# A hybrid two-layer backbone: the norms between the layers traced behind part of the next block's MLP products, and the first two projection groups ordered by block

## The chip, the cores and the metric

The kernel runs on one core of one Trainium2 chip. The metric is the device time of one execution in microseconds; the time shown is a median over several executions, and one further execution was profiled. PE is TensorE, ACT is ScalarE, DVE is VectorE, POOL is GpSimd, SP is the engine that issues most transfers.

## The reference

1,280 tokens (256 of context, then 1,024 latent ones) of width 1,024 pass through two layers. The reference in outline:

```python
for l in range(2):
    mod = silu(c) @ ada_w[l] + ada_b[l]          # shifts, scales, gates; one set for latent, one for context
    h = rms_norm(x, norm1_g[l]) * (1 + sc1) + sh1
    z = h @ w_in[l]                              # the projections: columns for four mixers
    mix = concat(s5(z), mlstm(z), diff_attention(z), gla(z)) @ w_out[l]
    x = x + g1 * mix
    h2 = rms_norm(x, norm2_g[l]) * (1 + sc2) + sh2
    x = x + g2 * (square(relu(h2 @ mlp_w1[l])) @ mlp_w2[l])
return rms_norm(x_latent, final_norm_g)
```

## The kernel before, in words

**Layout.** The stream X is kept with the 1,024 features on partitions (eight tiles of 128) and the tokens along the row, in three blocks: b0 is the context (tokens 0 to 255), b1 and b2 are 512 latent tokens each. Every float32 product is three products of reduced-precision halves (hi by hi, lo by hi, hi by lo: lines 1126 to 1128), so each weight tile is split into whi (a cast on ACT, line 1117) and wlo (a subtraction on DVE, line 1118), and each activation into hhi and hlo.

**Between the layers.** In the last pass of layer 0's MLP (w2, products named m2p) the blocks come in the order b1, b2, b0 (LAST). For each block there are G = 2 loads of weights, and M = 4 outputs for each load, of six matmuls each. Before the change, when a block's eight outputs are done, its X is stored (xl_d) and it is normed for layer 1 at once: block_rstd squares the eight tiles on ACT (nsq, line 1183), sums them on PE with eight small products (np4, line 1185), copies (line 1187), spreads by one product (npm, line 1189) and takes the inverse root (lines 44 to 49). norm_block then makes hhi and hlo: for odd tiles POOL multiplies (line 1201), ACT scales and casts (1205, 1206) and DVE subtracts (1207); for even tiles DVE multiplies (1210), ACT casts (1211) and DVE subtracts (1212).

**The projections.** z_steps goes through a list of groups (ZORD). In layer 0 the first are dak1, dak2, daq1; in layer 1 s50, s51, dak1. Each group has one weight tile of 128 columns and makes, per block, 24 matmuls into one PSUM bank (zp; the tag has two buffers), which ACT copies out into a tile "zst" and stores. The tiles zst, nsq and nt (line 1210) share one tag of two buffers. Before, a group passes over all blocks (b0, b1, b2 in layer 0; b1, b2, b0 in layer 1) before the next group. In layer 0 the norm of the blocks is traced between the split of the first group's weights and the first products, and rows of the modulation (adap, adar, lines 1161 to 1172) are woven in. `ready(("dak1",))` traces groups until the named one is done; after it the S5 mixer's preparation (s5_prep) is traced.

**What sets the order.** Each engine works through its instructions in order. The order on PE is not simply the traced order: PE's instructions are moved ahead or behind by a scheduler when the kernel is built, so that a product that would wait lets others pass, within the number of PSUM buffers. ACT and DVE stay close to the traced order.

Of the kernel before, what the change touches and what calls it, by code (L numbers as in the profile page):

```python
# [1095 lines left out]
BLK = [(0, 256), (256, 768), (768, 1280)]  # L1096
# [80 lines left out]
def block_rstd(env, P, x, n, ahead=1, own=True):  # L1177

    nc = env.nc
    p4 = env.bank("nm", "np4")  # L1180
    for k in range(8):
        sq = P.tile([128, 512], F32, tag="sq", name="nsq", bufs=2) if own else env.wp.tile([128, 512], F32, tag="zst", name="nsq", bufs=2)
        nc.scalar.activation(sq[:, :n], x[:, k], AF.Square)
        j = k % 4
        nc.tensor.matmul(p4[32 * j:32 * j + 32, :n], env.ones32, sq[:, :n], start=k < 4, stop=k >= 4, tile_position=(0, 32 * j))  # L1185
    s4 = P.tile([128, 512], F32, tag="rs_u", name="ns4", bufs=1)
    nc.scalar.copy(s4[:, :n], p4[:, :n])
    pm = env.bank("nm", "npm")
    nc.tensor.matmul(pm[:, :n], env.sel128, s4[:, :n], start=True, stop=True)
    return rstd_wide(env, P, pm[:, :n], n, ahead=ahead)  # L1190


def norm_block(env, P, x, y, n, sc, sh, hi, lo, room=None):

    nc = env.nc
    for k in range(8):
        if y is None or room and k % 2:
            t = x[:, k]
            if y is not None:
                t = room()[:, :n]  # L1200
                nc.gpsimd.tensor_tensor(t, x[:, k], y, op=ALU.mult)
            if y is None and k % 2:
                nc.vector.tensor_scalar(t, t, sc[:, k:k + 1], sh[:, k:k + 1], op0=ALU.mult, op1=ALU.add)
            else:
                nc.scalar.activation(t, t, AF.Identity, scale=sc[:, k:k + 1], bias=sh[:, k:k + 1])
            nc.scalar.copy(hi[:, k], t)
            nc.vector.tensor_tensor(lo[:, k], t, hi[:, k].bitcast(F32), op=ALU.subtract)  # L1207
            continue
        t = P.tile([128, 512], F32, tag="zst", name="nt", bufs=2)
        nc.vector.scalar_tensor_tensor(t[:, :n], x[:, k], sc[:, k:k + 1], y, op0=ALU.mult, op1=ALU.mult)  # L1210
        nc.scalar.activation(hi[:, k], t[:, :n], AF.Identity, bias=sh[:, k:k + 1])
        nc.vector.scalar_tensor_tensor(lo[:, k], t[:, :n], sh[:, k:k + 1], hi[:, k].bitcast(F32), op0=ALU.add, op1=ALU.subtract)
# [55 lines left out]
def tile_hybrid_backbone(ctx: ExitStack, tc: tile.TileContext, io, out):  # L1268
    nc = tc.nc
# [45 lines left out]
    def mod(l, part, s):  # L1315
        return mods[l][:, 8 * part:8 * part + 8, s]
# [9 lines left out]
    def z_steps(names, l, hh, zd):  # L1326

        def split(nm):
            if nm in ZT:
                return [split_w(env, io["wz"][l, ZT.index(nm)], 1024)]  # L1330
            src = io["wn"][l, ZN.index(nm)]
            return [split_w(env, src[:, 1024 * i:1024 * i + 1024], 1024) for i in range(2)]
        w = split(names[0])
        yield 0
        for i, nm in enumerate(names):
            if l == 0 and i >= 2:
                ahead(later, 1)
            early = i + 1 < len(names) and nm in ZT and names[i + 1] in ZT
            nw = split(names[i + 1]) if early else None
            blocks = range(1, 3) if (l == L - 1 and nm in LAT_ONLY) else FIRST[l]  # L1340
            yield from z_group(env, nm, w, hh, zd, blocks)
            traced.add(nm)
            if i + 1 < len(names):
                w = nw or split(names[i + 1])
# [21 lines left out]
    for l in range(L):  # L1366
# [198 lines left out]
        for g in range(32 // G):  # L1565
            hid = []
            for f in range(G):
                wh, wl = (w.rearrange("p (k c) -> p k c", k=8) for w in split_side(io["w1"][l, G * g + f]))
                hhi = P.tile([128, T], F32R, tag="hhi", name="hidhi", bufs=G + 1)
                hlo = P.tile([128, T], F32R, tag="hlo", name="hidlo", bufs=G + 1)  # L1570
                for b in blocks:
                    t0, t1 = BLK[b]
                    n = t1 - t0
                    p = acc("m1p")
                    mm3(nc.tensor, p[:, :n], [((wh[:, k], wl[:, k]), (H[b][0][:, k], H[b][1][:, k])) for k in range(8)])
                    rl = env.wp.tile([128, 512], F32, tag="zst", name="rl", bufs=2)
                    nc.scalar.activation(rl[:, :n], p[:, :n], AF.Relu)  # L1577
                    nc.vector.tensor_tensor(rl[:, :n], rl[:, :n], p[:, :n], op=ALU.mult)  # L1578
                    nc.scalar.copy(hhi[:, t0:t1], rl[:, :n])
                    nc.vector.tensor_tensor(hlo[:, t0:t1], rl[:, :n], hhi[:, t0:t1].bitcast(F32), op=ALU.subtract)  # L1580
                hid.append((hhi, hlo))
            M = 8 // G
            w2 = lambda i, split: (w.rearrange("p (m k c) -> p m k c", m=M, k=G) for w in split(io["w2"][l, G * g + i]))
            if g < 32 // G - 1:
                for i in range(G):
                    wh, wl = w2(i, split_side)
                    for mi in range(M):
                        for b in blocks:
                            down(wh, wl, mi, M * i + mi, b, hid)
            else:  # L1590
                if need:
                    for gen, _ in side:
                        list(gen)
                    for i in range(2):
                        make_scale(l + 1, i)
                    shut(spc)
                shut(h2c)
                if need:
                    hpc, hh = normed(l + 1)
                    spare, turn2 = [P.tile([128, T], F32R, tag=nm, name="spare", bufs=G + 1).bitcast(F32) for nm in ("hhi", "hlo")], [0]  # L1600

                    def room():
                        turn2[0] += 1
                        return spare[turn2[0] % 2][:, 512 * (turn2[0] // 2 % 2):512 * (turn2[0] // 2 % 2) + 512]
                for b in LAST[l]:
                    n = BLK[b][1] - BLK[b][0]
                    for i in range(G):
                        wh, wl = w2(i, split_side)
                        for mi in range(M):
                            down(wh, wl, mi, M * i + mi, b, hid)  # L1610
                    if need:
                        nc.sync.dma_start(xl_d[:, :, BLK[b][0]:BLK[b][1]], X[b])
                        y = block_rstd(env, NX, X[b], n, 1, False)
                        norm_block(env, env.wp, X[b], y, n, scl[l + 1][:, 0, b == 0], mod(l + 1, 0, b == 0), *hh[b], room)
        shut(hdc)
    fnc, P = pool("fin")
    for b in blocks:
# [97 lines left out]
```

## Time and profile before

| | |
|---|---|
| median of three executions | 3638.7 us (3633.97 to 3651.09) |
| the profiled execution | 3642.66 us, of which the span of instructions is 3640.9 us |
| mean granted PE clock | 0.953 of full |
| PE busy | 3387.3 us, 93% |
| DVE busy | 2170.0 us, 60% |
| ACT busy | 1308.3 us, 36% |
| POOL busy | 447.0 us, 12% |

The span runs from the first to the last instruction; 1.8 us lie outside it. An engine's busy time is the union of its instructions.

### The profile page before, as it was taken

What the parts mean: (1) busy time and instruction counts of PE and PEld (TensorE: products, weight loads), DVE (VectorE), ACT (ScalarE), POOL (GpSimd) and SP (SyncE); (2) the same over time, 40 slices, a digit from 0 to 9 for tenths busy, and PEclk for the clock granted to TensorE, in tenths of its full rate; (3) what the DMA queues carried; (4) which work ended last, traced back from release to release, by engine and by line L of the source; (5) the groups of instructions that cost most, each with busy time, mean ns of one, the idle gap of its engine ahead of it and who ended that gap; (6) DMA issues with size and microseconds to landing.
All of it is one profiled execution on the core that took longest, in us unless ns stands there. A gap on an engine that the chain in (4) does not pass through costs nothing. (4 is left out here: it accounts for less than half of the span.)

```text
span 3640.9 us, 58642 instructions
## 1 busy us (share of the span) xinstructions
PE 3387.3 (93%) x22810; PEld 2688.7 (74%) x22810; DVE 2170.0 (60%) x5479; ACT 1308.3 (36%) x2493; POOL 447.0 (12%) x520
## 2 busy tenths in 40 slices
PE   6989998799889999999999798999889999999998
PEld 3867767577657888888888476877677588888885
DVE  9664656788748865455544647475788643333334
ACT  4223435566632121212121522345676522222223
POOL 2131221222100000000000114130222000000000
PEclk8989989799999999999999999988899999999999
DMA  5675325665652222222111265324665411111112
GB/s 220 235 225 156 123 80 142 212 204 176 212 187 70 80 84 74 82 77 82 64 38 44 99 189 181 114 74 148 223 190 200 159 41 52 47 49 50 47 52 76
DMA packets 242173, 442.12 MB, mean 121 GB/s; under 512 B 48438, under 2 KB 141030, under 8 KB 241638
## 3 DMA queue, kind: packets, MB, share of 16 engines
q1 hardware_dynamic: 200998, 392.57, 33.5%
q10 hardware_dynamic: 35520, 30.52, 2.6%
q0 software_dynamic: 5376, 15.28, 1.2%
q8 instruction: 180, 2.95, 0.3%
q14 instruction: 99, 0.81, 0.1%
HBM read 328.42 MB, written 109.86 MB: 120 GB/s over the span
## 5 line engine op out<-in xcount | busy, mean ns | idle before, releaser
L1564 DVE SCALAR_TENSOR_TENSOR X<-m2p,mods,X 128x256 f32<-128x256 f32 (+1 forms) x512 | 345.9, 683 | 348.0 <-PE m2p L1128 347.1
L1117 ACT CAST whi<-raw 128x1024 fp32r<-128x1024 f32 x182 | 191.1, 1050 | 908.4 <-PE m2p L1127 644.7
L1126 PE MATMUL m2p<-hidhi,whi 128*128 128x512 f32 (+1 forms) x1280 | 473.6, 372 | 1.5 <-DVE rs_u L47 0.6
L1126 PE MATMUL m1p<-h2hi,whi 128*128 128x512 f32 (+1 forms) x1280 | 473.2, 370 | 0.0
L1128 PE MATMUL m2p<-hidhi,wlo 128*128 128x512 f32 (+1 forms) x1280 | 471.7, 370 | 1.1 <-DVE wlo L1118 1.1
L1127 PE MATMUL m2p<-hidlo,whi 128*128 128x512 f32 (+1 forms) x1280 | 472.4, 369 | 0.0
L1127 PE MATMUL m1p<-h2lo,whi 128*128 128x512 f32 (+1 forms) x1280 | 471.1, 368 | 0.0
L1128 PE MATMUL m1p<-h2hi,wlo 128*128 128x512 f32 (+1 forms) x1280 | 470.5, 368 | 0.0
L1118 DVE TENSOR_TENSOR wlo<-raw,whi 128x1024 fp32r<-128x1024 f32 x182 | 224.8, 1236 | 316.1 <-ACT whi L1117 298.8
L1126 PEld LDWEIGHTS m2p<-hidhi,whi 128*128 128x128 f32 x1280 | 241.3, 189 | 58.4 <-issue 9.5
L1126 PEld LDWEIGHTS m1p<-h2hi,whi 128*128 128x128 f32 x1280 | 241.0, 188 | 46.7 <-ACT whi L1117 4.2
L1128 PEld LDWEIGHTS m2p<-hidhi,wlo 128*128 128x128 f32 x1280 | 240.9, 188 | 46.7 <-issue 3.4
L1127 PEld LDWEIGHTS m2p<-hidlo,whi 128*128 128x128 f32 x1280 | 241.3, 188 | 41.9 <-issue 2.2
L1127 PEld LDWEIGHTS m1p<-h2lo,whi 128*128 128x128 f32 x1280 | 241.3, 188 | 41.5 <-issue 1.3
L1128 PEld LDWEIGHTS m1p<-h2hi,wlo 128*128 128x128 f32 x1280 | 241.1, 188 | 39.9
L1126 PE MATMUL zp<-hhi,whi 128*128 128x512 f32 (+1 forms) x664 | 257.8, 388 | 12.8 <-ACT zst L1239 9.6
L1127 PE MATMUL zp<-hlo,whi 128*128 128x512 f32 (+1 forms) x664 | 254.5, 383 | 8.6 <-DVE hlo L1207 8.1
L489 DVE TENSOR_SCALAR_CACHE_REDUCE das<-daps 128x512 f32<-128x512 f32 (+1 forms) x400 | 226.1, 588 | 51.2 <-PE daps L488 50.2
L1128 PE MATMUL zp<-hhi,wlo 128*128 128x512 f32 (+1 forms) x664 | 255.6, 385 | 0.0
L1578 DVE TENSOR_TENSOR rl<-rl,m1p 128x256 f32<-128x256 f32 (+1 forms) x160 | 100.7, 630 | 168.5 <-ACT rl L1577 168.4
L1126 PE MATMUL zp<-whi,hhi 128*128 128x256 f32 x624 | 183.4, 295 | 4.9 <-ACT whi L1117 4.8
L500 ACT ACTIVATE das<-das,danm 128x1280 f32<-128x1280 f32 x128 | 174.3, 1362 | 25.6 <-DVE danm L498 25.1
(459 smaller groups left out, 6484.8 us busy)
## 6 DMA issues: line engine op xcount, KB each, us to landing
raw<-w SPq DMA_DIRECT2D x136, 512.0 KB
adaw<-ada_w SPq DMA_DIRECT2D x96, 512.0 KB
whl<-wsp SPq DMA_DIRECT2D x80, 512.0 KB
daqk<-da_st SPq DMA_DIRECT2D x32, 640.0 KB
wsp<-whl SPq DMA_DIRECT2D x32, 512.0 KB
raw<-wz SPq DMA_DIRECT2D x30, 512.0 KB
mlE<-ml_rows SPq DMA_DIRECT2D x16, 640.0 KB
xn<-xo SPq DMA_DIRECT2D x72, 128.0 KB
```

What stands on the lines that cost most here:

```text
L489: v.tensor_scalar(s[:, a:b], p[:, 0:b - a], -1.0, None, op0=ALU.mult, op1=ALU.min, accum_out=pm[:, i:i + 1])
L500: act.activation(s[:, :k1], s[:, :k1], AF.Exp, bias=nm[:, 0:1], scale=-1.0, accum_out=sm[m])
L1117: nc.scalar.copy(hi, raw)
L1118: nc.vector.tensor_tensor(lo, raw, hi.bitcast(F32), op=ALU.subtract)
L1126: pe.matmul(out, ah, bh, start=i == 0, stop=False)
L1127: pe.matmul(out, ah, bl, start=False, stop=False)
L1128: pe.matmul(out, al, bh, start=False, stop=i == n - 1)
L1564: nc.vector.scalar_tensor_tensor(X[b][:, m], p[:, :n], mod(l, 5, s)[:, m:m + 1], X[b][:, m], op0=ALU.mult, op1=ALU.add)
L1578: nc.vector.tensor_tensor(rl[:, :n], rl[:, :n], p[:, :n], op=ALU.mult)
```

## The change

Two edits. In z_steps the weights of the first two groups are both split first, and then for each block both groups' products are made; `traced` learns of both at once, and only then are the third group's weights split and the old loop entered. This holds for both layers. In the last MLP pass, the store and norm of a block (now `normal(b)`) is traced after the first of the two weight loads of the next block's products; the last block's norm comes at the end, as before.

```diff
         w = split(names[0])
         yield 0
+
+        w1 = split(names[1])
+        for b in FIRST[l]:
+            for nm, x in zip(names, (w, w1)):
+                yield from z_group(env, nm, x, hh, zd, [b])
+        traced.update(names[:2])
+        w = split(names[2])
         for i, nm in enumerate(names):
-            if l == 0 and i >= 2:
+            if i < 2:
+                continue
+            if l == 0:
                 ahead(later, 1)
...
+                def normal(b):
+                    n = BLK[b][1] - BLK[b][0]
+                    nc.sync.dma_start(xl_d[:, :, BLK[b][0]:BLK[b][1]], X[b])
+                    y = block_rstd(env, NX, X[b], n, 1, False)
+                    norm_block(env, env.wp, X[b], y, n, scl[l + 1][:, 0, b == 0], mod(l + 1, 0, b == 0), *hh[b], room)
+
+                before = None
                 for b in LAST[l]:
-                    n = BLK[b][1] - BLK[b][0]
                     for i in range(G):
                         wh, wl = w2(i, split_side)
                         for mi in range(M):
                             down(wh, wl, mi, M * i + mi, b, hid)
-                    if need:
-                        nc.sync.dma_start(xl_d[:, :, BLK[b][0]:BLK[b][1]], X[b])
-                        y = block_rstd(env, NX, X[b], n, 1, False)
-                        norm_block(env, env.wp, X[b], y, n, scl[l + 1][:, 0, b == 0], mod(l + 1, 0, b == 0), *hh[b], room)
+                        if i == G // 2 - 1 and before is not None:
+                            normal(before)
+                    before = b if need else None
+                if need:
+                    normal(before)
```

What that does to the order on the engines, at three places. The first is PE between the layers, where block b1's last output (m2p_20082 in both) ends. Before, b1's sums follow at once:

```order
L1127 MATMUL m2p_20082<-hidlo_19906,whi_20054 128x512
L1128 MATMUL m2p_20082<-hidhi_19905,wlo_20055 128x512
L1185 MATMUL np4_20091<-nsq_20092,ones32_73 32x512
L1185 MATMUL np4_20091<-nsq_20095,ones32_73 32x512
L1126 MATMUL m2p_20174<-hidhi_19807,whi_20162 128x512
L1127 MATMUL m2p_20174<-hidlo_19808,whi_20162 128x512
```

After the change four outputs of b2 stand between them (the first is m2p_20096, the last m2p_20120, six matmuls of 512 columns each); here the last rows of them and b1's sums, now named np4_20129:

```order
L1126 MATMUL m2p_20120<-hidhi_19905,whi_20092 128x512
L1127 MATMUL m2p_20120<-hidlo_19906,whi_20092 128x512
L1128 MATMUL m2p_20120<-hidhi_19905,wlo_20093 128x512
L1185 MATMUL np4_20129<-nsq_20130,ones32_73 32x512
L1185 MATMUL np4_20129<-nsq_20133,ones32_73 32x512
L1126 MATMUL m2p_20212<-hidhi_19807,whi_20200 128x512
L1127 MATMUL m2p_20212<-hidlo_19808,whi_20200 128x512
```

So 24 matmuls have moved ahead of b1's sums. Further on, still on PE, the end of b0's sums (np4_20383) and its spread (npm_20410). Before, the last products of the first group for b2 are woven into the sums, and b0's products for that group (hhi0) follow:

```order
L1185 MATMUL np4_20383<-nsq_20396,ones32_73 32x256
L1185 MATMUL np4_20383<-nsq_20399,ones32_73 32x256
L1127 MATMUL zp_20515<-hlo2_20011,whi_20475 128x512
L1128 MATMUL zp_20515<-hhi2_20010,wlo_20476 128x512
L1185 MATMUL np4_20383<-nsq_20402,ones32_73 32x256
L1185 MATMUL np4_20383<-nsq_20405,ones32_73 32x256
L1189 MATMUL npm_20410<-ns4_20408,sel128_71 128x256
L1126 MATMUL zp_20543<-hhi0_20006,whi_20475 128x256
L1127 MATMUL zp_20543<-hlo0_20007,whi_20475 128x256
```

After the change b0's eight sums stand alone, and what follows npm_20410 is the first group's products for b2 (hhi2):

```order
L1185 MATMUL np4_20383<-nsq_20399,ones32_73 32x256
L1185 MATMUL np4_20383<-nsq_20402,ones32_73 32x256
L1185 MATMUL np4_20383<-nsq_20405,ones32_73 32x256
L1189 MATMUL npm_20410<-ns4_20408,sel128_71 128x256
L1126 MATMUL zp_20543<-hhi2_20010,whi_20475 128x512
L1127 MATMUL zp_20543<-hlo2_20011,whi_20475 128x512
L1128 MATMUL zp_20543<-hhi2_20010,wlo_20476 128x512
```

The copies out of PSUM (zst, line 1239) of the first group's first bank stand on ACT at the same place in both, behind all but one of b0's casts.

The second place is PE at the start of layer 0. Names: whi_383 and wlo_384 are the weights of dak1, whi_461 and wlo_462 those of dak2; hhi0 and hhi1 are blocks b0 and b1. Before, b1's 24 products with dak1 begin in the middle of b0's and run on; the rows after b0's last ones:

```order
L1128 MATMUL zp_465<-hhi0_375,wlo_384 128x256
L1126 MATMUL zp_465<-hhi0_375,whi_383 128x256
L1127 MATMUL zp_465<-hlo0_376,whi_383 128x256
L1128 MATMUL zp_465<-hhi0_375,wlo_384 128x256
L1127 MATMUL zp_493<-hlo1_378,whi_383 128x512
L1128 MATMUL zp_493<-hhi1_377,wlo_384 128x512
L1164 MATMUL adap_993<-adaw_994,cst_87 32x512
L1126 MATMUL zp_493<-hhi1_377,whi_383 128x512
```

After, the products of dak2 with b0 stand there, and all but two of dak1 with b1 behind them:

```order
L1128 MATMUL zp_465<-hhi0_375,wlo_384 128x256
L1164 MATMUL adap_639<-adaw_640,cst_87 32x512
L1164 MATMUL adap_639<-adaw_642,cst_87 32x512 x2
L1126 MATMUL zp_493<-hhi0_375,whi_461 128x256
L1127 MATMUL zp_493<-hlo0_376,whi_461 128x256
L1126 MATMUL zp_521<-hhi1_377,whi_383 128x512
L1127 MATMUL zp_521<-hlo1_378,whi_383 128x512
L1128 MATMUL zp_493<-hhi0_375,wlo_462 128x256
L1126 MATMUL zp_493<-hhi0_375,whi_461 128x256
L1127 MATMUL zp_493<-hlo0_376,whi_461 128x256
```

So 22 of the 24 products of 512 columns with dak1 and b1 moved behind dak2's products with b0.

The third place is DVE in the S5 mixer of layer 0 (s5W is line 365's work tile, daa and dax the rotary of the attention's inputs). Before, no rotary instruction stands between these rows:

```order
L376 TENSOR_TENSOR s5X_2108<-s5W_2118,s5t1_2120 128x160
L377 TENSOR_TENSOR s5X_2108<-s5W_2118,s5t1_2120 128x160
L365 TENSOR_TENSOR s5W_2172<-s5V_2169,s5tbl_2162 128x320
L318 SCALAR_TENSOR_TENSOR s5Y_2205<-U_1962,dsk_1961,s5py_2207 128x160
L367 TENSOR_TENSOR s5W_2172<-s5W_2172,s5t1_2174 128x160
L368 TENSOR_TENSOR s5W_2172<-s5W_2172,s5t1_2174 128x160
L371 SCALAR_TENSOR_TENSOR s5Z_2173<-r8_1960,s5W_2172 128x159 x2
```

After, the rotary of 384 columns does:

```order
L368 TENSOR_TENSOR s5W_2172<-s5W_2172,s5t1_2174 128x160
L371 SCALAR_TENSOR_TENSOR s5Z_2173<-r8_1960,s5W_2172 128x159 x2
L438 TENSOR_TENSOR daa_2244<-dax_2241,rope_2036 128x384
L373 TENSOR_TENSOR s5W_2172<-s5Z_2173,s5tbl_2162 128x320
L322 TENSOR_TENSOR s5y2_2228<-s5y2_2228,s5Y_2205 128x320
```

That unit (four such operations, a cast's subtraction and two POOL products) stood ahead of the S5 mixer's first s5W before.

## Rows read from the trace of the kernel before

**Rows 1.** The page: the span, and TensorE's busy time, share and instructions.

```profile
span 3640.9 us, 58642 instructions
...
PE 3387.3 (93%) x22810; PEld 2688.7 (74%) x22810; DVE 2170.0 (60%) x5479; ACT 1308.3 (36%) x2493; POOL 447.0 (12%) x520
```

**Rows 2.** Windows between the layers: start:end, length, then busy by engine, granted clock, DMA.

```profile
2032.30:2049.30 17.00, 8.12 (x35) 6.13 (x33) 15.25 (x20) 12.14 (x18) 5.90 (x4) 0.89 0.00 1
...
2049.30:2061.60 12.30, 11.62 (x38) 4.20 (x38) 5.20 (x8) 4.89 (x8) 0.00 (x0) 0.87 0.74 256
...
2061.60:2079.40 17.80, 14.45 (x66) 10.42 (x66) 15.04 (x19) 11.53 (x18) 6.39 (x4) 1.00 0.27 88
...
2086.30:2096.60 10.30, 0.70 (x2) 0.30 (x2) 6.83 (x14) 6.47 (x16) 3.45 (x6) 0.68 0.04 9
```

**Rows 3.** Waits of PE between the layers: us in total, times, longest.

```profile
PE zp L1126 <- ACT zst L1239: 9.6, 1, 9.6
...
PE np L1185 <- ACT nsq L1183: 8.9, 1, 8.9
```

**Rows 4.** Timeline of PE between the layers: start, us, line, operation, idle before.

```profile
2021.03 1.05 PE L1185 MATMUL np<-nsq,ones 128*32 128x512 f32 x4
...
2086.31 0.70 PE L1189 MATMUL npm<-ns,sel 128*128 128x256 f32 x2 [0.46 <-ACT ns L1187]
...
2096.65 0.58 PE L1126 MATMUL zp<-hhi,whi 128*128 128x256 f32 x1 [9.63 <-ACT zst L1239]
```

**Rows 5.** Timeline of ACT between the layers.

```profile
2048.67 0.61 ACT L1183 ACTIVATE nsq<-X 128x512 f32<-128x512 f32 x1
...
2096.03 0.56 ACT L1239 COPY zst<-zp 128x512 f32<-128x512 f32 x1
```

**Rows 6.** Timeline of DVE between the layers.

```profile
2037.92 3.09 DVE L1210 SCALAR_TENSOR_TENSOR nt<-X,scl,rs_y 128x512 f32<-128x512 f32 x2
...
2066.24 1.22 DVE L1118 TENSOR_TENSOR wlo<-raw,whi 128x1024 fp32r<-128x1024 f32 x1
...
2075.73 1.40 DVE L1210 SCALAR_TENSOR_TENSOR nt<-X,scl,rs_y 128x512 f32<-128x512 f32 x2
```

**Rows 7.** Timeline of POOL between the layers.

```profile
2037.47 5.90 POOL L1201 TENSOR_TENSOR spare<-X,rs_y 128x512 f32<-128x512 f32 x4 [107.68 <-DVE rs_y L49]
```

**Rows 8.** Timeline of PE at the start of layer 0.

```profile
78.34 0.28 PE L1128 MATMUL zp<-hhi,wlo 128*128 128x256 f32 x1
...
78.46 0.40 PE L1127 MATMUL zp<-hlo,whi 128*128 128x512 f32 x1
...
78.69 0.40 PE L1128 MATMUL zp<-hhi,wlo 128*128 128x512 f32 x1
...
85.83 0.40 PE L1128 MATMUL zp<-hhi,wlo 128*128 128x512 f32 x1
...
88.38 0.50 PE L1126 MATMUL zp<-hhi,whi 128*128 128x512 f32 x1 [2.15 <-ACT zst L1246]
...
169.84 1.05 PE L1171 MATMUL adap<-selada,adar 128*128 128x2 f32 x8 [2.03 <-ACT adar L1168]
```

**Rows 9.** Timeline of ACT at the start of layer 0.

```profile
87.02 1.04 ACT L1117 CAST whi<-raw 128x1024 fp32r<-128x1024 f32 x1
```

**Rows 10.** Timeline of DVE in layer 0.

```profile
69.01 2.28 DVE L1118 TENSOR_TENSOR wlo<-raw,whi 128x1024 fp32r<-128x1024 f32 x1
...
88.46 1.23 DVE L1118 TENSOR_TENSOR wlo<-raw,whi 128x1024 fp32r<-128x1024 f32 x1
...
187.53 1.37 DVE L440 TENSOR_TENSOR daa<-dax,rope 128x384 f32<-128x384 f32 x1
...
209.75 0.49 DVE L365 TENSOR_TENSOR s5W<-s5V,s5tbl 128x320 f32<-128x320 f32 x1 [19.72 <-ACT s5V L356]
```

**Rows 11.** Windows in layer 0, columns as in rows 2.

```profile
90.00:100.00 10.00, 10.00 (x50) 8.60 (x49) 10.00 (x49) 1.91 (x3) 2.63 (x5) 0.84 0.86 281
...
208.50:310.00 101.50, 86.97 (x640) 63.18 (x640) 79.99 (x193) 31.33 (x72) 39.73 (x57) 0.83 0.62 201
```

## The prediction

> **What bounds the kernel now.** I read the page first: PE is busy 3387.3 of 3640.9 us [rows 1], 93%, so the kernel is bound by PE, and a reordering can win only what PE waits, or loses to a low clock, in the places whose order changes. The two orders differ in two stretches alone: the start of layer 0 and the joint between the layers. I then read the windows of the joint, which show where PE is idle. The stretch from b1's first sum to the restart of the projections runs from 2021.03 to 2096.65 [rows 4], 75.6 us. In it PE is idle 8.9 us of 17.0 during b1's norm, 0.7 us in b2's sums, 3.4 us of 17.8 during b2's norm and 9.6 us of 10.3 during b0's [rows 2], some 22.5 us in all. The list of waits names two large ones: 8.9 us on the first square of b2, and 9.6 us on a copy out of PSUM [rows 3]. The timeline of ACT says why they are there. b2's first square runs at 2048.67, and the copy that frees the projections' bank at 2096.03 [rows 5], each behind the whole norm of the block before it on ACT. While norms run, DVE is busy 15.2 of 17.0 and 15.0 of 17.8 us, ACT 12.1 and 11.5 [rows 2]. So the joint is a chain of three norms on ACT and DVE, one after another, with PE's products as filler, of which there is 22.5 us too little.
>
> **The change: the joint.** It changes what lies beside the chain, and when the chain begins; the number of norms in it, and the place of the freeing copy on ACT, stay.
>
> (a) The chain begins later. Four outputs of b2 now come ahead of b1's sums on PE, 24 matmuls of 512 columns. Two starts of such matmuls lie 0.23 us apart (78.46, 78.69 [rows 8]), so b1's sums begin 24 x 0.23 = 5.5 us later: **+5.5**.
>
> (b) The products woven between b1's sums become narrower: eight of them have 256 columns now, at 0.12 us a start (78.34 to 78.46 [rows 8]) instead of 0.23: 8 x 0.11 = **-0.9**. Between b2's sums it is the other way round: 16 of 512 columns (3.7 us) where there were 22 of 256 (2.6 us): **+1.1**. In b0's sums ten projections of 512 columns fall away (2.3 us). The squares on ACT and PE's small products pace each other there, so I count a third: **-0.8**.
>
> (c) The norms themselves have the same instructions. One split of weights moves from b2's norm (its wlo, 1.22 us at 2066.24 [rows 6]) into b1's, where it stands among POOL's products, 5.90 us from 2037.47 [rows 7]. Beside POOL a DVE operation with two inputs takes longer: the pair of line 1210 takes 3.09 us at 2037.92, and 1.40 us at 2075.73, after POOL has ended [rows 6]; a wlo that began while POOL ran took 2.28 us against 1.23 [rows 10]. So b1's norm pays 2.3 at most, less what already lies in DVE's gaps (17.0 - 15.2 = 1.8), b2's saves 1.2: **0**, between -1.2 and +1.1. The Trainium skill, "SBUF — State Buffer", section "Who interferes with whom", describes the lock behind this as exclusive, the loser blocked fully rather than slowed. By that rule the wlo would wait out a whole POOL product, 5.90 / 4 = 1.5 us, and the sum would be 0.4 higher than by the row's 2.28; the rows, where both engines go on at about half speed, decide here.
>
> The joint's sum: 5.5 - 0.9 + 1.1 - 0.8 = **+4.9 us**. What is late next is the restart: the 5.5 us that PE has worked off earlier are not on the path of the chain, so they come back as idle time in front of later norms (PE has two PSUM buffers for projections, and now fills them with both groups of b1 instead of the first group's b1 and b2). After the restart the same amount is left on PE in both orders: three groups' worth of blocks less the 48 matmuls of 512 columns that were made. The bounds: +6 if none of (b) comes, and -22.5 if all the idle time were covered. The chain is the nearest row to what happens, so I take +4.9.
>
> **The change: the start of layer 0.** Before, PE made dak1's 24 products for b1 while ACT and DVE were still norming (the last at 85.83), waited 2.15 us and went on at 88.38 [rows 8]. Dak2's weights were cast only at 87.02 for 1.04 us [rows 9], and their wlo made from 88.46 to 89.69 [rows 10]. Now PE's order has dak2's products with b0 ahead of all but two of dak1's with b1, so PE stands until these weights exist, with 22 matmuls of 512 columns behind it that were done before. Before, from 88.38 on: dak1 b2, dak2 b0, b1 and b2, 3 x 24 x 0.23 + 24 x 0.12 = 19.4 us, and the window 90 to 100 has a clock of 0.84 [rows 11], which costs 1.6 us: end at 109.4. Now from 89.69 on: 22 x 0.12 + 22 x 0.23 + 72 x 0.23 = 24.3, and 1.6 again: 115.6. **+6.2**, bounded below by 0 (if PE had been made to wait there anyway) and above by +8 (if the longer rest of PE makes the low clock cost twice the 1.6 us). From there to the S5 mixer PE is nearly always busy, so the shift travels; one wait on it goes: PE waits 2.03 us at 169.84 for a copy (adar) behind a cast of the rotary on ACT [rows 8], and that copy now stands ahead of the cast: **-2.0**.
>
> The rotary unit of 384 columns now falls into the S5 mixer: four DVE operations of at most 1.37 us [rows 10], 5.5 at most, 2.2 at their length without POOL. Before, they lay ahead of a gap of 19.72 us in which DVE did nothing [rows 10]; now they lie in a stretch where DVE is busy 80.0 of 101.5 us and PE 87.0 [rows 11]. With no row for the wait that they make, I take half of their likely 3 us: **+1.5**, between 0 and +5.5. The start's sum: 6.2 - 2.0 + 1.5 = **+5.7**. The cover of both edits is spent: what was hidden behind norming is now in front of or behind it.
>
> **The sum.** 4.9 + 5.7 = 10.6 us on the profiled execution's 3642.7: 3653.3. That execution lies 4.0 us above the median of the runs shown, so against the median of 3638.7 the forecast is **3649 us**, 0.3% more. A measurement of this kernel can tell about 0.5%, 18 us, from no change.
>
> **Rivals.** *The waits in the joint are really covered.* The edit puts products between a block's end and its norm. If the scheduler's order let PE work through b1's norm (8.9 us) without pushing the freeing copy back, 8 to 18 us of rows 3 would go: with 5.7 lost at the start, -3 to -13: 3626 to 3636. For it speaks that the idle time is there and is large; against it that the copy still stands behind b0's norm on ACT, and that the order puts more, not less, in front of b1's sums.
>
> *The start costs nothing.* If the last transfers and the copies behind the norming end later than I think in both kernels, or the S5 stage waits for something that doesn't move, the 6.2 us are swallowed by 160 us; then only the joint counts: 3642 to 3645. Against it speaks that the order ahead of the mixer holds the same products as before, so nothing there shrinks to make room.
>
> *The S5 mixer of layer 0 stretches; this one ends slower.* The rotary, its casts and its POOL products now lie among DVE's scans, with PE's readout waiting behind each. The place is 208 to 310 us: PE is already idle 14.5 us there and the clock is 0.83 [rows 11], which is 17 us of lost pace. If the rotary takes all its 5.5 us on the chain, and two more stretches of 10 us fall to half clock, that is 5.5 + 10 against the 1.5 counted: +14 on the forecast, 3663. It decides once the mixer's stage is longer by over 9 us than before.
>
> *The change does not do what it says.* The norm of a block is traced behind products, yet on ACT, DVE and PE its chain is as long as before; that is the forecast itself, not a rival to it.
>
> **How the numbers follow.** The forecast, 3644 to 3654, 0.5; the joint covered 0.15; the start free 0.15; the mixer stretched 0.2. To reach faster by over 0.5% (under 3620.5) the whole 22.5 us would have to go with a free start: 0.06. Slower by over 0.5% (above 3656.9) is most of the last rival: 0.17. Within: 0.77. The range that leaves out no more than 2 in 10 drops the lower half of the covered joint and the upper part of the stretched mixer: 3630 to 3664.
>
> **What would show it.** In the joint: b1's first sum some 5.5 us later, the wait of the projections for the copy (line 1239) still there at about 10 us or more, the restart about 5 us later. If that wait is under 3 us, the joint is wrong. At the start: a wait of PE on line 1118's or 1117's weights of dak2 near 88 to 90 us, dak2's last product near 115 instead of 109, no wait on adar. In the mixer: its 101.5 us grown by 1 to 3; if it grew by 10, the third rival holds. If the S5 mixer starts at the old time, the start was free.

## The result, and the profile after

The changed kernel takes 3660.5 us (median of 5; 3657.0 to 3669.7) where the kernel before takes 3638.7 (median of 5). The ratio is 1.0054, with a 95% interval of 1.0040 to 1.0069: half a per cent slower, some 20 us. The profiled execution lies higher than the median, as it did before, and its span against [rows 1] is 25.9 us longer. The page of the kernel after:

```profile
span 3666.8 us, 58638 instructions
...
PE 3392.4 (93%) x22810; PEld 2691.4 (73%) x22810; DVE 2175.2 (59%) x5479; ACT 1308.3 (36%) x2493; POOL 450.4 (12%) x520
```

Where the time went is read by matching the instructions of PE in the two traces: for the same product of the same tile, how much later it starts. The lag is +2.4 us when the S5 mixer of layer 0 begins, +13.7 us at its last product, +15.2 us through the MLP of layer 0, and +21.9 us behind the joint between the layers. The mixer grew by 11.3 us, the joint with the products ahead of it by 6.7. Between these, in the mixers behind S5, two executions differ by several microseconds even where the order is the same. In the profiled run of the moved norms alone, whose layer 0 has the old order, the lag wandered by 9 us there, and in the changed kernel it fell from 13.7 to some 7 us and rose again to 15. The 4 us that the changed kernel's profile adds in layer 1's mixers are within that and are not explained here.

**The start of layer 0**, PE, answering to [rows 8]: the last product of dak1 with b0, the wait on dak2's weights, the first product that needs their wlo, and dak2's last product.

```profile
78.91 0.28 PE L1128 MATMUL zp<-hhi,wlo 128*128 128x256 f32 x1
...
83.98 0.78 PE L1164 MATMUL adap<-adaw,cst 128*32 128x512 f32 x2 [3.81 <-DMA adaw<-ada_w]
...
88.45 0.58 PE L1126 MATMUL zp<-hhi,whi 128*128 128x256 f32 x1 [2.84 <-ACT whi L1117]
...
90.08 0.58 PE L1128 MATMUL zp<-hhi,wlo 128*128 128x256 f32 x1
...
115.89 0.39 PE L1128 MATMUL zp<-hhi,wlo 128*128 128x512 f32 x1
```

PE now waits 2.84 us for the cast and starts again at 88.45, but with b1's 22 products still to do. Dak2 ends at 115.89; in the trace of before that product starts at 109.14.

**The S5 mixer of layer 0.** Its first product to its last on PE, first in the kernel before (a shorter window than in [rows 11]), then after:

```profile
208.50:303.40 94.90, 80.37 (x567) 56.81 (x567) 77.83 (x187) 28.96 (x67) 38.69 (x55) 0.82 0.64 210
```

```profile
210.90:317.10 106.20, 83.46 (x575) 58.22 (x575) 84.58 (x192) 29.77 (x68) 43.75 (x57) 0.82 0.69 225
```

The stage takes 106.2 us where it took 94.9. PE is idle 22.7 us in it instead of 14.5, at the same clock of 0.82; DVE is busy 6.8 us more and POOL 5.1. What PE waits for there, from the list of waits of the kernel after (in total, times, longest):

```profile
PE s5py L315 <- DVE s5X L376: 7.7, 3, 4.3
...
PE adap L1164 <- DMA adaw<-ada_w: 6.1, 3, 4.1
...
PE s5py L315 <- DVE s5X L381: 4.1, 4, 2.1
...
PE s5py L310 <- DVE s5Y L318: 1.9, 4, 0.7
```

Two operations of the third rotary unit, on DVE, and on SP the loads for it and the modulation's weights behind them:

```profile
229.13 1.28 DVE L438 TENSOR_TENSOR daa<-dax,rope 128x384 f32<-128x384 f32 x1
...
255.45 0.82 DVE L438 TENSOR_TENSOR daa<-dax,rope 128x640 f32<-128x640 f32 x1
```

```profile
221.04 0.42 SPq L432 DMA_DIRECT2D dax<-z_daq  x1
...
228.10 1.55 SPq L1161 DMA_DIRECT2D adaw<-ada_w  x1
```

In the kernel before the third unit ran at 185 to 189 us [rows 10]; now it runs from 229 on, among the scans.

**The joint**, PE, answering to [rows 4]: first sums and spreads of b1, b2 and b0, and the restart.

```profile
2041.62 0.62 PE L1185 MATMUL np<-nsq,ones 128*32 128x512 f32 x2
...
2052.47 0.70 PE L1189 MATMUL npm<-ns,sel 128*128 128x512 f32 x1
...
2071.02 1.06 PE L1185 MATMUL np<-nsq,ones 128*32 128x512 f32 x1 [4.17 <-ACT nsq L1183]
...
2084.53 0.59 PE L1189 MATMUL npm<-ns,sel 128*128 128x512 f32 x1
...
2102.02 0.64 PE L1185 MATMUL np<-nsq,ones 128*32 128x256 f32 x1 [6.44 <-ACT nsq L1183]
...
2108.02 0.48 PE L1189 MATMUL npm<-ns,sel 128*128 128x256 f32 x1 [0.46 <-ACT ns L1187]
...
2118.34 0.80 PE L1126 MATMUL zp<-hhi,whi 128*128 128x512 f32 x1 [9.63 <-ACT zst L1239]
```

From b1's first sum to the restart it takes 76.7 us; before, 75.6. The wait for the copy is as long as it was, 9.63 us. DVE in b1's norm, answering to [rows 6]:

```profile
2059.18 1.65 DVE L1210 SCALAR_TENSOR_TENSOR nt<-X,scl,rs_y 128x512 f32<-128x512 f32 x1
...
2062.82 1.89 DVE L1118 TENSOR_TENSOR wlo<-raw,whi 128x1024 fp32r<-128x1024 f32 x1
```

DVE between the inverse root's last two operations in b1's norm (lines 48 and 49), before and then after; L1573 is the addition of the MLP's outputs to X, line 1564 before:

```profile
2036.17 0.43 DVE L48 TENSOR_SCALAR rs_u<-rs_u 128x512 f32<-128x512 f32 x1
2036.64 0.69 DVE L49 TENSOR_TENSOR rs_y<-rs_y,rs_u 128x512 f32<-128x512 f32 x1
```

```profile
2056.74 0.42 DVE L48 TENSOR_SCALAR rs_u<-rs_u 128x512 f32<-128x512 f32 x1
2057.52 0.75 DVE L1573 SCALAR_TENSOR_TENSOR X<-m2p,mods,X 128x512 f32<-128x512 f32 x1 [0.36 <-PE m2p L1128]
2058.19 0.68 DVE L49 TENSOR_TENSOR rs_y<-rs_y,rs_u 128x512 f32<-128x512 f32 x1
```

And the copy on ACT, answering to [rows 5]:

```profile
2117.73 0.56 ACT L1239 COPY zst<-zp 128x512 f32<-128x512 f32 x1
```

### The profile page after: what moved, and what is told of

Read it like the earlier page. It is cut to its first block, busy times and chain, and to the rows that moved or that the text cites. A ratio compares the mean times of both kernels' runs of the same rounds, so it can differ in the third digit from the quotient of the medians.

```text
span 3666.8 us, 58638 instructions
## 1 busy us (share of the span) xinstructions
PE 3392.4 (93%) x22810; PEld 2691.4 (73%) x22810; DVE 2175.2 (59%) x5479; ACT 1308.3 (36%) x2493; POOL 450.4 (12%) x520
## 5 line engine op out<-in xcount | busy, mean ns | idle before, releaser
L1573 DVE SCALAR_TENSOR_TENSOR X<-m2p,mods,X 128x256 f32<-128x256 f32 (+1 forms) x512 | 345.8, 683 | 352.7 <-PE m2p L1128 351.8
L1127 PE MATMUL zp<-wlo,hhi 128*128 128x256 f32 x624 | 181.5, 291 | 3.7 <-DVE wlo L1118 2.4
```

The costliest lines, as they stand in the source:

```text
L1127: pe.matmul(out, ah, bl, start=False, stop=False)
L1573: nc.vector.scalar_tensor_tensor(X[b][:, m], p[:, :n], mod(l, 5, s)[:, m:m + 1], X[b][:, m], op0=ALU.mult, op1=ALU.add)
```

## The experiments

Each kernel was timed against the kernel before in five rounds on one chip. The ratios are of those runs; the stages are read from one profile each. "Stage" is the time from the S5 mixer's first product on PE to its last, in layer 0.

| kernel | ratio to before (95%) | mixer starts | stage | b1's first sum to restart |
|---|---|---|---|---|
| before | 1 | 208.5 | 94.9 | 75.6 |
| the change | 1.0054 (1.0040 to 1.0069) | 210.9 | 106.2 | 76.7 |
| norms moved alone | 1.0032 (1.0017 to 1.0047) | 209.7 | 96.2 | 78.3 |
| start by block alone | 1.0040 (1.0025 to 1.0054) | 210.1 | 106.5 | 76.0 |
| layer 1 by block alone | 1.0007 (0.9991 to 1.0023) | 209.6 | 94.0 | 77.6 |
| norms moved, layer 1 by block | 1.0024 (1.0009 to 1.0039) | 206.0 | 99.3 | 76.8 |
| start by block, queries' rotary behind | 1.0024 (1.0010 to 1.0039) | 211.1 | 104.6 | 75.9 |
| layer 1 by block, copies ahead | 1.0003 (0.9986 to 1.0019) | 205.9 | 93.5 | 87.7 |
| before, queries' rotary behind | 0.9970 (0.9955 to 0.9984) | 208.6 | 85.7 | 76.2 |
| copies ahead, norms moved | 1.0008 (0.9994 to 1.0023) | 207.3 | 92.7 | 86.2 |
| start by block, rotary's loads by POOL | 1.0038 (1.0025 to 1.0051) | 209.9 | 107.9 | 76.5 |
| before, rotary behind, loads by POOL | 0.9973 (0.9957 to 0.9988) | 206.7 | 84.4 | 76.0 |
| start by block, no modulation in the mixer | 1.0122 (1.0099 to 1.0144) | 226.2 | 96.2 | 76.0 |
| before, no modulation in the mixer | 1.0078 (1.0054 to 1.0102) | 225.1 | 85.1 | 75.6 |

**Taking the change apart.** Four kernels: the moved norms with the old z_steps; block by block for one layer with the old norms (the edit below, with `l == 0` or `l == 1`); and the moved norms with `l == 1`.

```diff
         w = split(names[0])
         yield 0
+        byblock = l == 0
+        if byblock:
+            w1 = split(names[1])
+            for b in FIRST[l]:
+                for nm, x in zip(names, (w, w1)):
+                    yield from z_group(env, nm, x, hh, zd, [b])
+            traced.update(names[:2])
+            w = split(names[2])
         for i, nm in enumerate(names):
+            if byblock and i < 2:
+                continue
```

> Only the norm of a block between the layers is moved behind half of the next block's last products; the projections keep the old order in both layers. Theory (the chain of three norms simply begins later, and b1's norm gets a second weight split among its work): the joint costs +6.5 us as in the changed kernel, layer 0 stays at 0: +5 to +8 us in all, the wait of the projections for the copy out of PSUM stays at about 9.6 us. Rival (the joint's loss comes from the block-by-block order, which needs b1's second weights during the norm): 0 to +2 us.

> Only layer 0's first two projection groups go block by block; norms and layer 1 as before. Theory (the start loses some 2.4 us and the S5 mixer of layer 0 stretches by some 10): +10 to +14 us, and a trace whose S5 stage begins some 2.4 us later and ends some 12 us later. Rival (the stretch of the S5 mixer is chance between two executions): +2 to +4 us.

> Only layer 1's first two projection groups go block by block; norms and layer 0 as before. Theory (the freeing copy stands behind b0's norm whichever group fills the two banks): -1 to +2 us, with the 9.6 us wait still there. Rival (the order by block changes the mixers of layer 1, which were 4 us later in the changed kernel's trace): +3 to +6 us.

> The change without its effect on layer 0: norms moved, and block by block in layer 1 alone. Theory (terms add): +5 to +8 us. Rival (the mixers of layer 1 lose as well): +10 to +12 us.

Both halves of the change are slow by themselves: the norms moved by 0.32%, the start by 0.40%, and layer 1's order by block by nothing that can be told from zero. The two parts that make up the change (the start by block; the norms moved with layer 1 by block) come to 0.40 + 0.24 = 0.64% against the whole's 0.54%, within their intervals. The medians of the first, second and fourth run (some 12, 15 and 9 us) lie above the ranges expected of them (5 to 8, 10 to 14 and 5 to 8); the intervals reach into the ranges, and what is over is not explained here. With layer 1's order alone the wait for the copy was 6.88 us and not the 9.6 expected, yet the joint took 2.0 us longer. The stage of the start alone repeats the 106 us to 0.3, and six profiles with the old order lie at 92.7 to 99.3, so its stretch is not chance. For the joint, each execution repeats itself closely. Moved norms alone, waits of PE from b1's sums to the restart:

```profile
PE zp L1126 <- ACT zst L1239: 9.6, 1, 9.6
...
PE zp L1126 <- ACT hhi L1211: 5.3, 1, 5.3
...
PE m2p L1128 <- DVE wlo L1118: 5.0, 1, 5.0
...
PE np L1185 <- ACT nsq L1183: 4.8, 3, 4.2
```

The wait for the copy is unchanged. Where 8.9 us were waited on b2's squares before, 4.8 us are waited on squares now, and two other waits of 5.3 and 5.0 us have come in. The products ahead of the joint (from the first of the MLP in layer 0 to b1's first sum) take 932.9 us before, 938.2 or 938.3 in all four profiled kernels with moved norms and 932.7 to 933.4 in the nine others: +5.4 us, the 24 matmuls.

**The copies ahead of b0's norm.** Is it the place of the freeing copy on ACT that holds PE? In two kernels (norms at the old place, and moved) layer 1's z_steps is made before b0's norm and traced through b1's two groups:

```diff
+                        if b == 0:
+                            zd = zalloc(l + 1)
+                            traced = set()
+                            rest = z_steps(ZORD[l + 1], l + 1, hh, zd)
+                            next(rest)
+                            ahead(rest, 18)
                         nc.sync.dma_start(xl_d[:, :, BLK[b][0]:BLK[b][1]], X[b])
                         y = block_rstd(env, NX, X[b], n, 1, False)
```

> Norms between the layers as before, start as before; layer 1's first two groups by block, and their products for b1 are traced ahead of b0's norm, so that the copies that free the two banks stand ahead of b0's norm on ACT. Theory (the place of that copy on ACT is what holds PE during b0's norm): 48 more matmuls of 512 columns fit before the restart, the 9.6 us wait falls to under 6, and the joint ends 6 to 10 us earlier than before: -5 to -10 us. Rival (the two copies and the second group's weight split lengthen the norms by as much): -2 to +3 us.

> As the run with copies ahead of b0's norm, and the norms moved behind half of the next block's products as in the change. Theory (the later begin of the chain, +5.4 us, and the longer norm of b1, +1.5, stay; the freed banks give some 10 back): -4 to 0 us against before, some 7 us above the run with the copies ahead and the norms at their old place. Rival (with the copies in place the moved norms cost nothing): -5 to -10 us.

48 more matmuls of 512 columns come before the restart and the wait there fell to 5.79 us. But a second wait for a freeing copy has come up ahead of it, so that PE waits 12.1 us for copies in all where it waited 9.63:

```profile
2073.30 0.80 PE L1126 MATMUL zp<-hhi,whi 128*128 128x512 f32 x1 [6.27 <-ACT zst L1239]
```

The joint became 12.1 us longer up to the restart, so 10.9 us of work done earlier brought nothing: the rival held (1.0003). The reason is on ACT (norms at the old place):

```profile
2081.32 0.59 ACT L1239 COPY zst<-zp 128x512 f32<-128x512 f32 x1 [7.55 <-PE zp L1128]
...
2081.80 0.42 ACT L1183 ACTIVATE nsq<-X 128x256 f32<-128x256 f32 x1
```

The second copy waits 7.55 us for its products, and b0's first square stands behind it in ACT's queue. The copies freed the banks and delayed the last norm by as much. With the norms moved as well the ratio was 1.0008; the intervals of the two overlap, so the difference between them is not measured; the 7 us that were expected between them did not show, though the chain again begins 5.4 us later.

**What stretches the S5 mixer.** First the rotary of the queries, traced behind the mixer, with the start by block and on the kernel before:

```diff
-        beside(both(s5_mix(...), 2, dap, 1), rest, 1300)
+        beside(both(s5_mix(...), 2, itertools.islice(dap, 2) if l == 0 else dap, 1), rest, 1300)
```

> Layer 0's start by block as in the run of the start alone, but in layer 0 the last two rotary units (the queries') are traced behind the S5 mixer instead of beside it: the 384-column unit moves to the mixer's last part on DVE, the 640-column one behind it. Theory (the rotary among DVE's scans is what stretches the S5 mixer by some 10 us): the stage loses at least 6 us of that, and the whole is +2 to +8 us against before. Rival (late weight loads and the clock stretch it): the stage stays some 10 us longer, the whole at +11 to +15.

> The kernel before, with the last two rotary units of layer 0 traced behind the S5 mixer; by the build's order only the 640-column unit leaves the mixer. Theory (rotary work among DVE's scans stretches the mixer): the stage from 208 to 310 us is 3 to 8 us shorter, -3 to -8 us in all. Rival (DVE has room there): -1 to +1 us.

On the kernel before, this is a gain, larger than expected: 0.9970, some 11 us, and a stage of 85.7 us. With the start by block the stage stayed at 104.6: the rival held there, though the whole (1.0024, some 9 us) lies between the two ranges. The edit put both units late into the mixer, not out of it:

```profile
271.21 0.52 DVE L439 TENSOR_TENSOR daa<-dax,rope 128x384 f32<-128x384 f32 x1
...
293.68 0.81 DVE L439 TENSOR_TENSOR daa<-dax,rope 128x640 f32<-128x640 f32 x1
```

and one of PE's long waits lies at such a place (6.56 us up to 296.06, on DVE's s5Y). The other, 5.50 us up to 264.48, ended before the first of the two units began, so it is not theirs. This run does not clear the rotary, and it does not convict it.

Then the loads of the rotary, issued by POOL in place of SP, again in both (on the kernel before together with the edit above):

```diff
-        nc.sync.dma_start(rt, rope)
+        q = nc.gpsimd if l == 0 else nc.sync
+        q.dma_start(rt, rope)
...
-                nc.sync.dma_start(x[:, 0, :n], zT(nm + "1")[:, t0:t1])
-                nc.sync.dma_start(x[:, 1, :n], zT(nm + "2")[:, t0:t1])
+                q.dma_start(x[:, 0, :n], zT(nm + "1")[:, t0:t1])
+                q.dma_start(x[:, 1, :n], zT(nm + "2")[:, t0:t1])
```

> Layer 0's start by block as in the run of the start alone; the rotary's loads in layer 0 (the table and the attention's inputs) are issued by POOL instead of SP, so they no longer stand behind the weight loads in SP's order, and the third rotary unit stands ahead of the mixer's first s5W again. Theory (SP's order brings those loads late, and with them the rotary, its stores and the later weight loads fall into the mixer): the mixer's stage on PE falls from 106 us to 94 to 98 (before 95), the whole to +2 to +6 us against before. Rival (the mixer is long because it begins in another state of the clock, whatever the loads do): the stage stays above 103, the whole at +11 to +15.

> The kernel before (no part of the change), with the last two rotary units traced behind the S5 mixer and the rotary's loads issued by POOL; in the build's order all four units then stand ahead of the mixer's first s5W on DVE. Theory (rotary work and its loads out of the mixer shorten it): a stage of 84 to 88 us against 95, -8 to -13 us in all, at least as good as the run with the units behind alone (-11). Rival (the first s5W now waits for the queries' products and loads): the stage begins 5 us or more later, -3 to +3 us in all.

On the kernel before all four units then ran ahead of the mixer on DVE, and the stage was the shortest of all, 84.4 us; the time is 0.9973, as good as the rotary behind alone and no better. With the start by block the first unit still began at 179.5 us. The third ran ahead of the mixer now, as it should; the fourth began at 218 in the mixer, where before it began at 242, and PE waited 8.94 us for DVE at one place:

```profile
195.54 0.56 DVE L439 TENSOR_TENSOR daa<-dax,rope 128x384 f32<-128x384 f32 x1 [4.10 <-DMA dax<-z_daq]
...
231.72 0.63 PE L310 MATMUL s5py<-U,s5toep 128*128 128x160 f32 x1 [8.94 <-DVE s5Y L318]
```

The stage stayed at 107.9 us, so this theory, that the late loads of the rotary on SP are the cause, fell in the form in which it was put. The run also shows that the stage can be as long with the third unit out of the scans. The rotary's stores stayed on SP.

Last, the modulation's rows beside the mixer traced later in both kernels, so that no load of their weights lies in it:

```diff
-            if l == 0 and i >= 2:
+            if l == 0 and (2 <= i < 6 or i >= 11):
                 ahead(later, 1)
```

> Layer 0's start by block as in the run of the start alone; the rows of the modulation that were woven into the groups beside the S5 mixer are traced later, so no load of their weights and no product of theirs lies in the mixer, while the rotary stays where the block order put it. Theory (SP's order brings these loads late in the mixer, PE waits for them and its clock falls): the stage falls from 106 us to 92 to 98 and lies at most 5 us above the same edit on the kernel before. Rival (the third rotary unit among DVE's scans is the cost): the stage stays 8 us or more above that of the same edit on the kernel before.

> The kernel before with the same edit: no rows of the modulation beside the S5 mixer. Theory (PE waited 3 us for such a load there and ran on at the low clock): the stage falls from 95 us to 86 to 92, the whole -2 to -8 us unless the rows cost as much where they go. Rival (they only filled PE's idle time): the stage stays at 94 to 96.

As a whole both are slower, against what was expected of the second (the mixer alone begins some 16 us later), but the stages tell the theories apart. Start by block, then the kernel before, each from the first product of its mixer to its last:

```profile
226.20:322.40 96.20, 60.71 (x498) 44.76 (x497) 80.17 (x188) 25.60 (x61) 44.33 (x57) 0.70 0.57 185
```

```profile
225.10:310.20 85.10, 59.39 (x503) 43.73 (x502) 76.22 (x183) 25.46 (x61) 40.80 (x55) 0.76 0.53 169
```

Both stages lost some 10 us, and the difference is 11.1 us, as it was with the loads in place (106.5 - 94.9 = 11.6). So the waits for the modulation's weights, 6.1 us in the list above, are not what makes the changed kernel's mixer longer. What is left in it is the third rotary unit, with DVE busy 4.0 us more and POOL 3.5 more, and what its loads and stores hold up.

**Where the mixer loses it.** This is read from the traces. The mixer makes eight passes (j in the kernel), with two pairs of scans each on DVE (line 371). Counted from the mixer's first product on PE, the scans of the third pass begin 3.2 us later than before, behind the third rotary unit's first operation; those of the fourth 6.8 us, those of the fifth 13.3, and so it stays, at 12 to 14, up to the last. The first scans of the fifth pass, before and after:

```profile
264.48 0.86 DVE L371 TENSOR_TENSOR_SCAN s5Z<-r,s5W 128x159 f32<-128x159 f32 x2
```

```profile
280.20 0.85 DVE L371 TENSOR_TENSOR_SCAN s5Z<-r,s5W 128x159 f32<-128x159 f32 x2
```

So only the first 3 to 4 us stand right behind the unit. Where the rest is added, the S5 mixer's own loads come late on SP: its matrix for the fourth pass (s5mi) and the eight loads for the fifth to the eighth (s5za). Before, and then after, with the first of the third unit's stores and with PE's wait:

```profile
232.36 0.43 SPq L338 DMA_DIRECT2D s5mi<-s_minT  x1
...
242.95 3.91 SPq L336 DMA_DIRECT2D s5za<-s_lag  x8
```

```profile
222.05 0.37 SPq L338 DMA_DIRECT2D s5mi<-s_minT  x1
...
237.10 0.38 SPq L449 DMA_DIRECT2D da_st<-dahi  x1
...
254.80 0.43 SPq L338 DMA_DIRECT2D s5mi<-s_minT  x1
...
257.27 2.31 SPq L336 DMA_DIRECT2D s5za<-s_lag  x5
...
268.20 2.22 SPq L336 DMA_DIRECT2D s5za<-s_lag  x3
```

```profile
258.53 1.31 PE L352 MATMUL s5pv<-U,s5mi 128*64 128x160 f32 x16 [1.12 <-DMA s5mi<-s_minT]
```

The third unit's four stores, which before were issued by 216 us, now stand ahead of these loads in SP's order, up to 242; the fourth unit's loads follow them at 242.27 (before, at 231.39), then a store of the mixer's own at 254.44, and the fourth unit's stores stand among the eight loads. The eight loads begin this long after the mixer's first product, with the stage behind it:

| kernel | eight loads begin | stage |
|---|---|---|
| before; the other five with its order in layer 0 | 34.5; 33 to 35 | 94.9; 92.7 to 99.3 |
| before, queries' rotary behind; with loads by POOL too | 18.8; 17.3 | 85.7; 84.4 |
| the change; start by block alone | 46.4; 44.3 | 106.2; 106.5 |
| start by block, rotary's loads by POOL | 48.9 | 107.9 |
| no modulation in the mixer: before; start by block | 18.8; 36.9 | 85.1; 96.2 |
| start by block, queries' rotary behind | 34.9 | 104.6 |

Apart from the last row, a later begin goes with a longer stage, on the whole. In the last the loads come as early as in the kernel before, and both units run late in the mixer instead. The loads also wait for the mixer itself, since their tile has one buffer, and no run moved them alone: that they are the larger part of the stretch is argued from the traces and not shown.

## Why the prediction came out as it did

The time lies in the range of 3630 to 3664. The forecast of its likeliest case, 3649, does not: of the named cases it was the stretched S5 mixer that came (3663), with a chance of 0.2. That its number fits is in part luck. The sum of the terms was 10.6 us, and they come to 20.2 in the profile (joint 6.5, start 2.4, mixer 11.3); the rival had put its 14 us together from the unit's own 5.5 us on the chain and 10 us of low clock, and neither came in that form.

*The joint, forecast +4.9, measured +6.5.* (a) The chain begins 5.4 us later, as worked out: the products ahead of it take 938.2 us instead of 932.9. (b) b1's sums are 0.4 us shorter (forecast 0.9), b2's 1.2 longer (1.1), b0's 0.9 shorter (0.8). (c) The norms were put at 0, between -1.2 and +1.1. b1's takes 18.55 us from its spread to b2's first sum against 17.05, b2's 17.49 against 17.79, b0's 10.32 against 10.34: +1.2, just above the upper end. The wlo that moved into b1's norm took 1.89 us beside POOL, not the 1.22 of [rows 6]; [rows 10] had 2.28. By the Trainium skill's "SBUF — State Buffer", section "Who interferes with whom", the wlo would have waited out a POOL product; the trace shows it prolonged by 0.67 us, less than that, which does not decide about the rule, since a product could have been part done when the wlo began. But the wlo is not where b1's norm lost its 1.5 us. From the spread to the inverse root's last operation (line 49), which stands ahead of the wlo and of POOL's first product, it takes 5.72 us instead of 4.35; from POOL's first product to b2's first sum it takes 12.01 instead of 11.87. Within the first stretch DVE now does two additions to X, of 0.48 and 0.75 us, between the inverse root's operations, and waits 0.36 us for the product of the second. They belong to the products that the moved norm is traced among. The three other kernels with moved norms show 5.69 to 5.72 us there. The term was put at nothing for a cost that did not come, and another came in its place; that the sum is nearly within the bounds is luck. The freeing copy still stands behind b0's norm and PE waits 9.63 us for it.

*The start, forecast +4.2 to the mixer, measured +2.4.* Dak2's last product comes at 115.89; worked out were 115.6. The wait on adar is gone, as said. The rest was given back on the way: in the kernel before the granted clock is 0.83 in the window 170 to 180 us, right behind that wait, which costs 1.7 us, and now it is 1.00 there. The start of the mixer varies by some 4 us between profiles, so 1.8 us of difference is not much.

*The rotary in the mixer, forecast +1.5, measured +11.3.* This is the step that failed in size: "I take half of their likely 3 us". The unit's four operations are only part of what it brings in: DVE is busy 6.8 us more in the changed kernel's mixer, with the casts' subtractions and the longer operations beside POOL, and the stage gained nearly twice that. The prediction priced the unit's time on DVE alone. The scans are 3.2 us late right behind the unit and 13.3 us two passes on, and between these the mixer's own loads come 12 to 20 us later on SP, behind the rotary's stores and loads: a path that the working did not have. The point from which the third rival decides, 9 us, was passed. Its clock part did not come: 0.82 in both. On the kernel before, a mixer without the queries' rotary among its first scans is 9.2 and 10.5 us shorter, with DVE 2.8 us more busy in the one and 3.3 less in the other, so a rotary unit there costs more than its own time on DVE. For the start by block the cause of the 11 us stays open. All five kernels with that start have the stretch, and the modulation's loads are excluded. The third unit's place on DVE is not needed for it: with the rotary's loads by POOL that unit ran ahead of the mixer, and the stage was 107.9 us, with the fourth unit among the first scans instead. The late loads fit four of the five and were not tried.

*What was not in the working.* That the first rotary unit would begin 20 us later, at 183 instead of 163 us, was seen on DVE's order alone as a unit that moves; that each of its stores and the next loads then stand later on SP, so that units follow each other into the mixer and stand ahead of the mixer's own loads, was not counted.

## What to carry to other kernels

To trace a stall's cause behind other work moves that work in front of it: when the waiting chain runs on other engines, its begin is put off by just what was placed ahead, and the stall comes back at its end. A copy that frees a buffer can be moved ahead in its engine's queue only as far as its own input is ready, since all behind it waits too. And a small unit pushed from a slack stretch into one where four engines hand work to each other should not be priced at its own busy time alone: its loads and stores take a place in the issuing engine's order as well, and what stands behind them comes later (here by 12 to 20 us; how much of the stage's 11 us that made was not tried). Here the better edit was the opposite one, to put such a unit behind the stage's first scans (0.9970).

## What the runs showed that was not expected

Moving one rotary unit of 640 columns from about 240 to 275 us in the kernel before shortened the S5 mixer's stage by 9.2 us; with it the granted clock in the stage rose from 0.82 to 0.90 (of 2.4 GHz, a mixture of its two levels, 2.4 and 1.2), and the mixer's own eight loads began 18.8 us after its first product instead of 34.5. Which of these made the gain was not tried apart. The stage's length also goes with the clock: with the old order in layer 0 it took 92.7 to 99.3 us in six profiles, and the longest of them, at a clock of 0.74, had less idle time on PE (12.2 us) than the one of 94.9 (14.5).

```profile
208.60:294.30 85.70, 74.48 (x563) 52.06 (x562) 80.61 (x187) 29.05 (x67) 39.81 (x54) 0.90 0.67 219
```
